# A router's ranking of tokens, cut into four groups instead of three, with four merge steps at each turn

## The chip, the cores and the metric

The kernel runs on one core of one Trainium2 chip. The metric is the device time of one execution in microseconds (us), as the median of several runs. The core has five engines that run side by side, each through its own list of instructions in order: TensorE (PE in the profile), VectorE (DVE), ScalarE (ACT), GpSimd (POOL) and SyncE (SP, which here only issues transfers). Transfers can be issued from SP, ACT and POOL.

## The reference

An encoder of two layers over 1024 tokens of 1024 channels. Each layer mixes tokens, projects the merged result with `w_out`, normalises it, and then lets each of 16 experts take the 128 tokens whose affinity to it is highest:

```python
x = layer_norm(DEEPNORM_ALPHA * x + mix, ln1_g[l], ln1_b[l])      # mix ends with merged @ w_out
...
cap = EC_FACTOR * T // N_EXPERTS                                   # 2 * 1024 // 16 = 128
aff = jax.nn.softmax(jnp.einsum('btd,de->bte', x, w_router).astype(jnp.float32), axis=-1)
gate, idx = lax.top_k(jnp.swapaxes(aff, 1, 2), cap)
xs = jax.vmap(lambda xb, ib: xb[ib])(x, idx)
hid = jax.nn.silu(jnp.einsum('becd,edf->becf', xs, w1)) * jnp.einsum('becd,edf->becf', xs, w3)
ye = jnp.einsum('becf,efd->becd', hid, w2) * gate[..., None].astype(x.dtype)
```

## The kernel before

The program is written out by Python generators, and the order in which they are advanced is the order of the instructions on each engine. `run` advances a main generator; after each of its turns it lets `W.step` load and split a weight piece, and `side_all` advance the work that follows. `side_all` takes one step of each generator in `posts`, and three rounds over the generators in `lows`.

`out_main` is the main generator here. It goes over eight token tiles of 128 tokens; each is projected by 16 turns of three matmuls of 512 columns (the products are split in three for accuracy, lines 325 to 327, output `pz`), and it yields after every second turn. L1269 adds the residual, and L1270 takes statistics. `turned` transposes a half of the tile on TensorE (L1240) and ScalarE copies it (L1242). `post` follows each tile: `ln_mv` finishes the statistics (lines 420 to 422, the last on GpSimd), `logits` (L1287) multiplies by the router's weights, `affinities` (L1294 to L1299) makes the softmax, and `ln_apply` writes the normalised rows, which are then stored twice (L1234, L1235; for the last tile L1234 is issued from ScalarE's queue).

`ln_apply` has a parameter `spread`: that many of the two halves go over ScalarE (L432) and two products on GpSimd (L433, L434); the others take two VectorE instructions (L436, L437).

`topk_stage` ranks. When the tiles of a group are done, two small matmuls put the group's affinities into rows of 64 values (L1343), and ScalarE copies them to a work buffer `tkb` (L1346). Eight rounds of L1354 (the eight largest) and L1357 (take them out) put each row in order. `moved` (L1330) brings rows together through TensorE and PSUM, L1360 or `join` (L1334) fetches them, and `ordered` puts a row in order in seven steps of two instructions (L1321 the larger, L1322 the smaller of each pair). Each `yield` ends a step. `lag` is six empty steps while the tiles still run. `TK` holds the 128 largest of each expert so far. After the last group L1370 takes the threshold, `topk` turns it into places, and the first expert's rows are gathered (L1446), transposed (L1461) and multiplied.

Of the kernel before, what the change touches and what calls it, by code (L numbers as in the profile page):

```python
# [22 lines left out]
NE = 16  # L23
# [60 lines left out]
class Weights:  # L84
    """Streams weight pieces: DMA in, split into two float32r parts."""

# [67 lines left out]
def tile_encoder_trunk(ctx: ExitStack, tc: tile.TileContext, I, out, dbg=None, depth=DEPTH):  # L154
# [23 lines left out]

# [1 line left out]
    cst = cp.tile([128, NCONST], F32, name="cst")  # L180
# [42 lines left out]

# [1 line left out]
    RT = dram([4, 128, RTW], "RT")  # L225
# [11 lines left out]

# [1 line left out]
    names = {}  # L239
# [46 lines left out]

# [1 line left out]
    sides, posts, lows = [], [], []  # L288
# [11 lines left out]
    def side_all():  # L300
        """one step of the first side that is ready, of each tile that follows, and of one of the low ones"""
        for g in list(posts):
            try:
                next(g)
            except StopIteration:
                posts.remove(g)
        for _ in range(3):
            for g in list(lows):
                try:
                    next(g)  # L310
                except StopIteration:
                    lows.remove(g)
        return [side_step(), bool(posts or lows)]
# [14 lines left out]

# [1 line left out]
    def bcast_row(dst, src, off, n, eng=None):  # L330
# [55 lines left out]

# [1 line left out]
    def alloc_xt():  # L388
        """x transposed in two float32r parts: [part][token half][pair of k] -> [128, 2, 512]"""
        return [[[slot([128, 2, 512], F32R, f"x{part}{hf}{i}") for i in range(4)] for hf in range(2)]  # L390
                for part in "hl"]
# [18 lines left out]

# [1 line left out]
    def ln_stats(z, eps):  # L412
# [12 lines left out]
    def ln_apply(zs, mv, g, b, o, spread=1):  # L425
        """halves: one on VectorE, the other shared by ScalarE and GpSimd (spread)"""
        if spread:
            nc.vector.scalar_tensor_tensor(mv[:, 2:3], mv[:, 0:1], -1.0, mv[:, 3:4], op0=OP.mult, op1=OP.mult)  # L428
        for hf in range(2):
            ns = slice(512 * hf, 512 * hf + 512)  # L430
            if spread and hf >= 2 - spread:
                nc.scalar.activation(o[:, ns], zs[hf], AF.Identity, scale=mv[:, 3:4], bias=mv[:, 2:3])  # L432
                nc.gpsimd.tensor_tensor(o[:, ns], o[:, ns], g[:, ns], op=OP.mult)  # L433
                nc.gpsimd.tensor_tensor(o[:, ns], o[:, ns], b[:, ns], op=OP.add)  # L434
            else:
                nc.vector.scalar_tensor_tensor(o[:, ns], zs[hf], mv[:, 0:1], g[:, ns], op0=OP.subtract, op1=OP.mult)  # L436
                nc.vector.scalar_tensor_tensor(o[:, ns], o[:, ns], mv[:, 3:4], b[:, ns], op0=OP.mult, op1=OP.add)  # L437
# [3 lines left out]

    # =====================================================================
    def pair(shape, name, dtype=F32):
        return [slot(shape, dtype, f"{name}{i}") for i in range(2)]

    def transposes_to(yt, src, hf):
        """src [128 t, 4, 256] token-major (half hf of the tokens) -> yt[ct][:, half]"""
        for ct in range(2):
            p = bank("py")
            for k in range(4):  # L450
                nc.tensor.transpose(p[:, 128 * k:128 * k + 128], src[:, k, 128 * ct:128 * ct + 128], ident)
            nc.scalar.copy(yt[ct][:, 512 * hf:512 * hf + 512], p)
        yield
# [77 lines left out]

# [1 line left out]
    def attention(l, L, T):  # L533
# [161 lines left out]

# [1 line left out]
    def mlstm(l, L, T):  # L697
        CV, GB = L["CV"], L["GB"]
        IGF, VV = T.pop("igf"), T.pop("cv")
        pre = [T.pop("cq"), T.pop("ck")]  # L700
        # gate rows [64 (dir, chunk, head), 128]
        nc.vector.tensor_tensor(IGF[:, 1], IGF[:, 1],
# [32 lines left out]
        for j in range(2):  # L735
            nc.tensor.transpose(p[0:1, 64 * j:64 * j + 64], gm[:, j:j + 1], ident[:64, :64])
        # chunk recurrence of the running maximum, rows ordered (dir, head, step)
        cr = sm.tile([1, 5, 64], F32, name="cr", tag="u0", bufs=1)
# [61 lines left out]
        yield  # L800
        # convolution and silu (twice the value), feature-major
        qk = []
# [19 lines left out]
        for hf in range(2):  # L822
# [6 lines left out]
            yield  # L829
        # states at the start of each chunk  # L830
        CS = pair([128, 8, 2, 65], "CS")
# [149 lines left out]

    # =====================================================================
    def mixers_main(l, L, T, XT, rows):
# [144 lines left out]
        del VV, IGF  # L1128
        # gates: tanh(z / 2)
        W.raw_max, W.prep_max = 1, 3  # L1130
# [58 lines left out]
    def out_main(l, L, MG, xsrc, R, nxt):  # L1189
        # the router takes rows before their normalisation: with weights times g, the sum of these, and b's part  # L1190
        CV, gw = L["CV"], L.pop("wr")
# [8 lines left out]
        L.update(gw=gw, gc=gc)  # L1200
        # twice the sum is normalised (MG holds twice the merged branches), with four times the epsilon
        LG = pair([128, D], "lg")
# [9 lines left out]
        def post(t, x, xt, st):  # L1212
            ts = slice(128 * t, 128 * t + 128)
            mv = ln_mv(st, 4.0 * EPS)
            if t == 0:
                p = bank("pl")
                nc.tensor.matmul(p[:, 0:2 * NE], ones, gs.rearrange("p a e -> p (a e)"), start=True, stop=True)
                nc.vector.tensor_copy(gc, p[:, 0:2 * NE].rearrange("p (a e) -> p a e", a=2))
            if t < 7:
                yield  # L1220
            if t == 0:
                turned(x, xt, 0)
                yield
            pl = bank("pl")
            logits(L, xt, pl, 0)
            turned(x, xt, 1)
            if t < 7:
                yield
            logits(L, xt, pl, 1)
            affinities(L, t, pl, mv, R)  # L1230
            for _ in range(6 if t == 7 else 0):
                yield
            ln_apply(halves(x), mv, LG[0], LG[1], x, spread=1 + (t > 5))
            (nc.scalar if t == 7 else nc.gpsimd).dma_start(X1[l][ts, :], x)  # L1234
            nc.gpsimd.dma_start(XA[l][ts, :], x)  # L1235
# [53 lines left out]
    def affinities(L, t, p, mv, R):  # L1289
        """of a token tile, from its rows before normalisation times the router's weights"""  # L1290
        AF_, gc = R[0], L["gc"]
# [7 lines left out]
        nc.vector.tensor_scalar(AF_[:, t, :], AF_[:, t, :], rs[:, 2:3], None, op0=OP.mult)  # L1299
        if t in (3, 5, 7):  # L1300
            lows.append(topk_stage(R, {3: 0, 5: 4, 7: 6}[t], t))

    def topk_stage(R, t0, t):
        """the values of token tiles t0..t: rows of 64 put in order, then rows joined (two rows, one of them
        reversed, fall and rise; the larger of each pair, 128 apart, are the 128 largest of two rows of 128);
        TK holds the 128 largest so far"""
        AF_, TK, stages = R
        nt = t + 1 - t0
        r = NE * nt
# [53 lines left out]
        if t == 7:  # L1363
            while stages[0] != t0:
                yield
            join(3, TK, TB[2], NE)
            q = moved(TB[2][:r], NE, NE)
            yield from ordered(3, NE)
            join(3, TB[4], q, NE)
            nc.vector.tensor_reduce(TK[:, 0:1], TB[3][:NE], axis=AX.X, op=OP.min)  # L1370
            return
# [19 lines left out]
    def topk(l, R):  # L1391
        """1 + place of each token among those its expert takes (0: not taken), ties by the lower index"""
        AF_, mn, _ = R
# [35 lines left out]
    def moe(l, pos, tail):  # L1429
# [67 lines left out]
        def h3_last(e):  # L1497
            """one half of the columns after the other, so that the first is turned behind the second"""
            p3 = [bank("h3"), bank("h3")]
# [108 lines left out]
    def add_first(zs, t):  # L1608
        """a token tile taken to PSUM"""
        p = [bank("pf"), bank("pf")]  # L1610
# [5 lines left out]
    def add_last(tail, t, nf, p, inside):  # L1616
        """what the last expert gives to a token tile, added in PSUM or to the tile"""
        zs, yeh, yel, ohT = tail[:4]
# [7 lines left out]
    def finish(l, tail):  # L1626
        """LN2 of one token tile at a time: statistics run one tile ahead"""
        zs, LG = tail[0], tail[4]
# [41 lines left out]

    # =====================================================================
    for l in range(depth):
# [87 lines left out]
```

The weights of the experts stream through 45 buffers of 512 KB; `W.budget` says how many pieces may be held.

## Time and profile before

| | us |
|---|---|
| median of 3 runs (lowest, highest) | 3269.47 (3265.74, 3276.28) |
| span of the profiled execution | 3270.7 |
| TensorE busy in it | 3073.0 (94%) |
| VectorE busy | 2154.1 (66%) |
| ScalarE busy | 1462.6 (45%) |
| GpSimd busy | 1319.3 (40%) |

The profiled execution is listed by its span alone: 3270.7 us, which lies 1.2 us over the median of the runs and inside their range. Its mean granted TensorE clock is 0.977. The two layers run the same code: the projection of layer 0 ends near 958 us and its first expert product starts at 994 us; in layer 1 the same places are 1612.5 us later. Busy time is a sum over stages with different limits, so what this change does is read from the stretch from 900 to 994 us and its twin.

### The profile page before, as it was taken

The page shows a single profiled execution, that of the slowest core. Times are in us where ns is not written, and L with a number is a line of the kernel's source. Part 1 is how long each engine was busy: PE and PEld are TensorE (multiplying, and loading weights), DVE is VectorE, ACT ScalarE, POOL GpSimd, SP SyncE. Part 2 cuts the span into 40 slices and gives each one's busy share as a digit, 9 for nine tenths or more (in the row PEclk, how much of TensorE's full clock was granted, in tenths as well). Part 3 has the DMA queues.
Part 4 walks back from the last instruction along what each step waited for, and adds up shares of the span by engine and source line. Part 5 has one row for each costly group of instructions (what it writes and reads, how often), then busy time and mean ns, then how long its engine had stood idle before and what let it go on. Part 6 is the DMA issues. An engine that isn't in the chain of part 4 may idle for free. (4 is left out here: it accounts for less than half of the span.)

```text
span 3270.7 us, 45191 instructions
## 1 busy us (share of the span) xinstructions
PE 3073.0 (94%) x15502; PEld 2452.3 (75%) x15502; DVE 2154.1 (66%) x3736; ACT 1462.6 (45%) x2101; POOL 1319.3 (40%) x1244
## 2 busy tenths in 40 slices
PE   8999999999978999999899999999999699999997
PEld 7977787778756777777689787877778477777774
DVE  3435552228679999999962465422385899999898
ACT  3122223332226777777531222233312277777773
POOL 0000011005436777777630000100074377777786
PEclk9999999999988999999999999999999799999998
DMA  4312323238567999999522123331484699999973
GB/s 162 97 33 78 110 90 126 65 105 298 197 238 256 358 356 346 354 360 355 164 94 85 39 84 103 123 100 59 163 297 147 237 338 358 352 351 359 356 286 123
DMA packets 283111, 670.64 MB, mean 205 GB/s; under 512 B 26866, under 2 KB 125258, under 8 KB 282880
## 3 DMA queue, kind: packets, MB, share of 16 engines
q1 hardware_dynamic: 259616, 586.16, 49.4%
q0 software_dynamic: 22976, 80.54, 8.3%
q8 instruction: 122, 2.00, 0.2%
q14 instruction: 109, 0.89, 0.1%
q10 hardware_dynamic: 288, 1.05, 0.1%
HBM read 578.60 MB, written 89.06 MB: 204 GB/s over the span
## 5 line engine op out<-in xcount | busy, mean ns | idle before, releaser
L131 DVE TENSOR_TENSOR wlo<-wraw,whi 128x768 fp32r<-128x768 f32 (+1 forms) x918 | 1161.6, 1296 | 483.9 <-ACT whi L124 456.7
L124 ACT CAST whi<-wraw 128x1024 fp32r<-128x1024 f32 (+1 forms) x922 | 944.2, 1047 | 362.0 <-PE h L326 81.3
L131 POOL TENSOR_TENSOR wlo<-wraw,whi 128x256 fp32r<-128x256 f32 x772 | 857.9, 1183 | 274.5 <-ACT whi L124 231.7
L325 PE MATMUL pb<-xh,whi 128*128 128x512 f32 x1344 | 549.3, 409 | 0.0
L326 PE MATMUL pb<-xl,whi 128*128 128x512 f32 x1344 | 529.5, 394 | 0.0
L327 PE MATMUL pb<-xh,wlo 128*128 128x512 f32 x1344 | 529.3, 394 | 0.0
L326 PE MATMUL h<-wlo,xsT 128*128 128x512 f32 x1024 | 414.6, 405 | 50.7 <-DVE wlo L131 34.2
L325 PE MATMUL h<-whi,xsT 128*128 128x512 f32 x1024 | 416.7, 407 | 0.5 <-ACT xsT L1464 0.5
L327 PE MATMUL h<-whi,xsT 128*128 128x512 f32 x1024 | 406.1, 397 | 5.4 <-DVE xsT L1465 5.4
L325 PEld LDWEIGHTS pb<-xh,whi 128*128 128x128 f32 x1344 | 252.9, 188 | 78.7 <-issue 21.8
L327 PEld LDWEIGHTS pb<-xh,wlo 128*128 128x128 f32 x1344 | 252.7, 188 | 58.7
L326 PEld LDWEIGHTS pb<-xl,whi 128*128 128x128 f32 x1344 | 253.2, 188 | 52.7 <-issue 1.9
L326 PEld LDWEIGHTS h<-wlo,xsT 128*128 128x128 f32 x1024 | 194.6, 190 | 126.1 <-DVE wlo L131 61.3
L1138 ACT ACTIVATE gt<-pb,CVh 128x512 f32<-128x512 f32 x128 | 87.6, 685 | 362.5 <-PE pb L327 341.0
L327 PEld LDWEIGHTS h<-whi,xsT 128*128 128x128 f32 x1024 | 194.2, 190 | 45.0 <-DVE xsT L1465 6.8
L326 PE MATMUL py<-wlo,hT 128*128 128x512 f32 x512 | 208.9, 408 | 19.5 <-POOL wlo L131 15.8
L325 PEld LDWEIGHTS h<-whi,xsT 128*128 128x128 f32 x1024 | 194.3, 190 | 41.3 <-ACT xsT L1464 1.5
L325 PE MATMUL py<-whi,hT 128*128 128x512 f32 x512 | 202.8, 396 | 0.0
L327 PE MATMUL py<-whi,hT 128*128 128x512 f32 x512 | 201.7, 394 | 0.0
L325 PE MATMUL pa<-whi,xh 128*128 128x256 f32 (+1 forms) x640 | 188.7, 295 | 6.7 <-ACT whi L124 5.8
L326 PE MATMUL pa<-wlo,xh 128*128 128x256 f32 (+1 forms) x640 | 186.2, 291 | 2.2 <-DVE wlo L131 2.2
L327 PE MATMUL pa<-whi,xl 128*128 128x256 f32 (+1 forms) x640 | 185.4, 290 | 0.1
(381 smaller groups left out, 4452.1 us busy)
## 6 DMA issues: line engine op xcount, KB each, us to landing
wraw<-in_w_e_dram SPq DMA_DIRECT2D x768, 512.0 KB
wraw<-in_w_in_dram SPq DMA_DIRECT2D x100, 512.0 KB
GD<-gt SPq DMA_DIRECT2D x64, 512.0 KB
gl<-GD SPq DMA_DIRECT2D x64, 512.0 KB
Rb<-RD POOLq DMA_DIRECT2D x32, 256.0 KB, 4.9
wraw<-in_w_branch_dram SPq DMA_DIRECT2D x16, 512.0 KB
wraw<-YT SPq DMA_DIRECT2D x16, 512.0 KB
wraw<-in_w_out_dram SPq DMA_DIRECT2D x16, 512.0 KB
```

The source lines that it names most:

```text
L124: self.nc.scalar.copy(hi, raw)
L131: e.tensor_tensor(lo[c], raw[c], hi[c].bitcast(F32), op=OP.subtract)
L325: nc.tensor.matmul(p, sh, mh, start=first, stop=False)
L326: nc.tensor.matmul(p, sh, ml, start=False, stop=False)
L327: nc.tensor.matmul(p, sl, mh, start=False, stop=last)
L1138: nc.scalar.activation(gt[:, 512 * hf:512 * hf + 512], p, AF.Tanh, scale=0.5, bias=CVh[:, j:j + 1])
```

## The change

`side_all` takes four rounds over `lows` instead of three. The groups of token tiles are 0 to 3, 4 to 5, 6, and 7 instead of 0 to 3, 4 to 5, and 6 to 7; the last group then has 16 rows of 64 for each half instead of 32, so its second joining is gone. The last tile's `ln_apply` stands directly behind its `affinities` (before, six turns later). Tile 6's normalisation goes whole to VectorE (`spread` 0, before 2); tile 7's keeps 2.

```diff
@@ side_all
-        for _ in range(3):
+        for _ in range(4):
             for g in list(lows):
@@ out_main, post
             affinities(L, t, pl, mv, R)
-            for _ in range(6 if t == 7 else 0):
-                yield
-            ln_apply(halves(x), mv, LG[0], LG[1], x, spread=1 + (t > 5))
+            ln_apply(halves(x), mv, LG[0], LG[1], x, spread={6: 0, 7: 2}.get(t, 1))
             (nc.scalar if t == 7 else nc.gpsimd).dma_start(X1[l][ts, :], x)
@@ affinities
-        if t in (3, 5, 7):
-            lows.append(topk_stage(R, {3: 0, 5: 4, 7: 6}[t], t))
+        if t in (3, 5, 6, 7):
+            lows.append(topk_stage(R, {3: 0, 5: 4, 6: 6, 7: 7}[t], t))
@@ topk_stage
             join(3, TK, TB[2], NE)
-            q = moved(TB[2][:r], NE, NE)
-            yield from ordered(3, NE)
-            join(3, TB[4], q, NE)
             nc.vector.tensor_reduce(TK[:, 0:1], TB[3][:NE], axis=AX.X, op=OP.min)
```

The other lines of the diff take out comments. What the generators make of it shows in the instruction lists. Line numbers from 1231 on are smaller by two in the changed kernel (by five from 1370 on).

On VectorE, at token tile 4 of layer 0: the end of the affinities, the normalisation of the half that VectorE takes (`xr`), and what stands behind it. Before:

```order
L1298 RECIPROCAL rs<-rs 128x1
L1299 TENSOR_SCALAR aff<-aff,rs 128x16
L428 SCALAR_TENSOR_TENSOR mv<-mv 128x1
L436 SCALAR_TENSOR_TENSOR xr<-xr,mv,lg_6438 128x512
L437 SCALAR_TENSOR_TENSOR xr<-xr,mv,lg_6439 128x512
L1269 SCALAR_TENSOR_TENSOR xr<-xr,pz 128x512
L1270 BN_STATS st<-xr 128x6
L1360 COPY tkb<-pl 64x64
L1321 TENSOR_TENSOR tkb<-tkb 64x64
```

The same place in the changed kernel:

```order
L1297 TENSOR_SCALAR aff<-aff,rs 128x16
L428 SCALAR_TENSOR_TENSOR mv<-mv 128x1
L436 SCALAR_TENSOR_TENSOR xr<-xr,mv,lg_6438 128x512
L437 SCALAR_TENSOR_TENSOR xr<-xr,mv,lg_6439 128x512
L1319 TENSOR_TENSOR tkb<-tkb 64x8x8
L1320 TENSOR_TENSOR tkb<-tkb 64x8x8
L1319 TENSOR_TENSOR tkb<-tkb 64x16x4
L1320 TENSOR_TENSOR tkb<-tkb 64x16x4
L1319 TENSOR_TENSOR tkb<-tkb 64x32x2
L1320 TENSOR_TENSOR tkb<-tkb 64x32x2
L1319 TENSOR_TENSOR tkb<-tkb 64x64
L1320 TENSOR_TENSOR tkb<-tkb 64x64
```

The first group's copy and first three steps have moved ahead of tile 4's affinities, and its last four steps now stand right behind the normalisation.

On TensorE, at token tile 6 of layer 0, behind the tile's logits (L1287 before, L1285 in the changed kernel): the projection of tile 7 (`pz`) and the small matmuls of the ranking. Before:

```order
L1287 MATMUL pl<-wr,xt 128x16 x4
L325 MATMUL pz<-whi,mh 128x512
L326 MATMUL pz<-wlo,mh 128x512
L327 MATMUL pz<-whi,ml 128x512
L325 MATMUL pz<-whi,mh 128x512
L326 MATMUL pz<-wlo,mh 128x512
L327 MATMUL pz<-whi,ml 128x512
L1330 MATMUL pl<-tkb,cst 32x64
L325 MATMUL pz<-whi,mh 128x512
```

In the changed kernel, from the end of the six products behind the same logits on:

```order
L1341 MATMUL pl<-cst,aff 16x64 x2
L325 MATMUL pz<-whi,mh 128x512
L326 MATMUL pz<-wlo,mh 128x512
L327 MATMUL pz<-whi,ml 128x512
L325 MATMUL pz<-whi,mh 128x512
L326 MATMUL pz<-wlo,mh 128x512
L327 MATMUL pz<-whi,ml 128x512
L1328 MATMUL pl<-tkb,cst 16x128
L325 MATMUL pz<-whi,mh 128x512
```

Tile 6's own affinities are now turned into rows here (L1341), and six products later stands the second joining of tiles 4 and 5 (L1328, 16x128), which before stood behind the whole projection. In the same way the first group's joining to 32 rows (32x128) now stands twelve products behind tile 4's logits; before it stood behind tile 5's transposes. Its row of 16x128 has moved up from behind tile 5's affinities to the stretch behind tile 5's first transposes. The rows of tiles 0 to 3 and of tiles 4 and 5 (L1343) are made six products behind their tile's logits, before twelve.

On ScalarE, at the end of the ranking of layer 0: the last tile's affinities, its normalisation, its store and the copy of the last group's rows. Before:

```order
L1297 ACTIVATE aff,rs<-rs 128x16
L1346 COPY tkb<-pl 64x64
L432 ACTIVATE xr<-xr,mv 128x512 x2
L1234 DMA X_115<-xr 128x1024
L124 CAST whi<-wraw 128x1024 x3
```

In the changed kernel:

```order
L1295 ACTIVATE aff,rs<-rs 128x16
L432 ACTIVATE xr<-xr,mv 128x512 x2
L1232 DMA X_115<-xr 128x1024
L1348 COPY tkb<-pl 16x64 x2
L124 CAST whi<-wraw 128x1024 x3
```

The copies from which the last group is put in order now stand behind the store of the normalised rows.

## Rows read from the trace of the kernel before

**Rows 1.** Windows: busy us of PE, PEld, DVE, ACT, POOL; clock, DMA share

```profile
899.80:961.50 61.70, 57.39 (x289) 45.63 (x289) 43.26 (x159) 13.13 (x31) 26.28 (x30) 0.94 0.57 212
935.40:941.10 5.70, 5.70 (x14) 4.46 (x14) 3.77 (x26) 0.00 (x0) 0.60 (x2) 0.50 0.47 184
2549.40:2552.30 2.90, 2.90 (x8) 2.27 (x7) 2.90 (x24) 0.00 (x0) 0.05 (x1) 0.50 0.91 362
981.50:994.10 12.60, 5.09 (x42) 4.17 (x42) 10.15 (x30) 1.63 (x2) 3.13 (x4) 0.50 0.15 43
1040.00:1560.00 520.00, 491.92 (x2267) 380.87 (x2265) 479.95 (x574) 391.46 (x433) 398.37 (x353) 1.00 0.98 355
```

**Rows 2.** TensorE's waits from 895 to 995 us: total us, times, longest

```profile
PE pl L1330 <- DVE tkb L1322: 10.1, 2, 7.1
...
PE pq L1240 <- DVE xr L1269: 0.7, 1, 0.7
```

**Rows 3.** Timeline of VectorE, tiles 4 and 5: start us, us, then the instruction

```profile
914.15 0.23 DVE L1294 SCALAR_TENSOR_TENSOR rs<-gc,mv,pl 128x16 f32<-128x16 f32 x1 [2.76 <-PE pl L1287]
...
917.27 0.68 DVE L1269 SCALAR_TENSOR_TENSOR xr<-xr,pz 128x512 f32<-128x512 f32 x1
...
932.02 1.28 DVE L1321 TENSOR_TENSOR tkb<-tkb 32x64 f32<-32x64 f32 x1
...
934.57 0.21 DVE L1322 TENSOR_TENSOR tkb<-tkb 32x64 f32<-32x64 f32 x1
```

**Rows 4.** Timeline of TensorE, tiles 4 and 5

```profile
913.97 0.48 PE L325 MATMUL pz<-whi,mh 128*128 128x512 f32 x1
...
915.21 0.39 PE L327 MATMUL pz<-whi,ml 128*128 128x512 f32 x1
...
934.92 0.58 PE L1330 MATMUL pl<-tkb,cst 32*16 32x128 f32 x2 [2.95 <-DVE tkb L1322]
```

**Rows 5.** Timeline of VectorE, tiles 5, 6 and 7

```profile
930.57 0.75 DVE L436 SCALAR_TENSOR_TENSOR xr<-xr,mv,lg 128x512 f32<-128x512 f32 x1
...
949.30 0.23 DVE L1294 SCALAR_TENSOR_TENSOR rs<-gc,mv,pl 128x16 f32<-128x16 f32 x1 [2.56 <-PE pl L1287]
...
950.75 0.23 DVE L1299 TENSOR_SCALAR aff<-aff,rs 128x16 f32<-128x16 f32 x1
...
957.69 0.21 DVE L1321 TENSOR_TENSOR tkb<-tkb 32x64 f32<-32x64 f32 x1
...
958.07 0.21 DVE L1321 TENSOR_TENSOR tkb<-tkb 32x64 f32<-32x64 f32 x1
```

**Rows 6.** Timeline of VectorE behind the last affinities

```profile
963.02 0.23 DVE L1299 TENSOR_SCALAR aff<-aff,rs 128x16 f32<-128x16 f32 x1
...
964.02 0.22 DVE L1354 MAX8 tkb<-tkb 64x8 f32<-64x64 f32 x1 [0.21 <-ACT tkb L1346]
...
969.99 0.21 DVE L1354 MAX8 tkb<-tkb 64x8 f32<-64x64 f32 x1
...
970.77 0.21 DVE L1360 COPY tkb<-pl 32x64 f32<-32x64 f32 x1 [0.45 <-PE pl L1330]
...
977.83 0.28 DVE L1334 TENSOR_TENSOR tkb<-TK,tkb 16x128 f32<-16x128 f32 x1
...
981.20 0.27 DVE L1370 TENSOR_REDUCE TK<-tkb 16x1 f32<-16x128 f32 x1
```

**Rows 7.** Timeline of ScalarE, tiles 6 and 7

```profile
951.14 1.52 ACT L432 ACTIVATE xr<-xr,mv 128x512 f32<-128x512 f32 x2 [0.61 <-issue]
...
971.52 1.52 ACT L432 ACTIVATE xr<-xr,mv 128x512 f32<-128x512 f32 x2 [7.53 <-DVE mv L428]
977.61 0.35 ACTq L1234 DMA_DIRECT2D X<-xr  x1
978.00 1.99 ACT L124 CAST whi<-wraw 128x1024 fp32r<-128x1024 f32 x2 [4.96 <-POOL xr L434]
```

**Rows 8.** Waits of SyncE's queue from 960 to 1040 us: total us, times, longest

```profile
SPq L103 <- DVE wlo L131: 37.4, 9, 28.1
```

## Prediction

> **What bounds the stretch now.** I first cut the execution into windows [rows 1]. While the last projection runs (899.8 to 961.5 us) TensorE is busy for 57.39 of 61.7 us: its queue sets the pace, and whatever makes it wait is lost. In the ranking behind it nearly nothing runs on TensorE, and the reader sees one chain instead: VectorE's merges up to the threshold, the places, the gather, and the first expert product at 994 us. The experts follow at 491.92 busy of 520 us. Next I read who makes TensorE wait near the ranking [rows 2]: its joinings (L1330) wait for the merges twice, 7.1 us at the end, where nothing else could run, and 2.95 us in the middle of the projection (the 10.1 less the 7.1), where products stand behind. The timelines [rows 3 to 7] say what each of these waits is made of. Layer 1 repeats layer 0, so every term counts twice.
>
> **The projection.** The lists show that the ranking's small matmuls now come earlier in TensorE's queue, so the question for each is whether VectorE has its rows ready. TensorE takes its matmuls in order: in the 2.95 us wait no product was run [rows 4].
>
> *The joining to 32 rows* now stands twelve products behind tile 4's logits. Tile 4's affinities begin on VectorE at 914.15, and the next row behind the normalisation starts at 917.27 [rows 3]. There the changed list has the last four merge steps. Two of them fall beside GpSimd's two products of that tile: the same situation at tile 5 took from 932.02 to 934.78, so 2.76 us for two pairs [rows 3], where a pair alone takes 0.38 (957.69 to 958.07) [rows 5]. VectorE is done at 917.27 + 2.76 + 0.76 = 920.79, and TensorE starts 0.14 later, as at 934.92 behind 934.78 [rows 3, 4]. Its own twelve products start at 913.97, at 0.25 a step (six of them up to 915.21) [rows 4], so that the twelfth ends near 917.1. New wait: 3.8 us. What goes is the 2.95 us of the joining to 16 rows: it now stands 24 products (6.0 us at 0.25) behind the one to 32, while VectorE needs seven pairs at 0.38 and tile 5's residual row (2.7 and some 1.4) for it.
>
> *The second joining of tiles 4 and 5*, before the first thing behind the projection, now stands twelve products behind tile 6's logits, and tile 6's normalisation is whole on VectorE in front of the merges it needs. Affinities at 949.30, their last row at 950.75; two such rows of 512 take 1.45 (930.57 to 932.02), four 2.9; then four pairs, no GpSimd product beside them, 1.5 [rows 3, 5]. With 0.15 for the end of the affinities VectorE is done at 955.3, and TensorE starts at 955.5. By tile 4's spacing its first six products are through at 950.8; it waits 0.3 for tile 6's affinities, takes 0.35 for L1343, and is through with the next six at 953.0. New waits: 0.3 + 2.5 = 2.8 us. What is late next is tile 7's projection.
>
> *Smaller terms.* Tiles 3 and 5 have their L1343 six products earlier too, at 0.35 of wait each: 0.7. Two more small groups lie inside the projection; taken at 0.35 each (bounds nothing, and the 0.58 that one takes [rows 4]): 0.7. The 0.7 us that tile 7's transposes waited for L1269 [rows 2] go, since VectorE is now ahead there. Ten merge rows now stand between the last statistics and their sum, 1.4 us at 0.14 each (42 rows from the first to the eighth maximum, 5.97 us [rows 6]); most hides behind the logits: 0.5.
>
> *The clock.* After its 2.95 us wait TensorE was granted 0.50, the lower level of 1.2 GHz, in layer 0 for 14 products in 5.70 us, in layer 1 for 8 in 2.90 [rows 1]. At 0.25 a product these lost 2.2 and 0.9 us. Now two waits of that kind stand in a layer instead of one. I add one such fall at 2.2, the larger, since the first wait is longer than the old one; bounds nothing and 3.5 (two of 2.2 less the old 0.9).
>
> Sum of the projection: 3.8 - 2.95 + 2.8 + 0.7 + 0.7 - 0.7 + 0.5 + 2.2 = 7.05 us later per layer.
>
> **Behind the last affinities.** Call the start of their last row X, before 963.02; the threshold was at 981.20, 18.2 later [rows 6]. Removed are the last joining, its seven steps and its maximum, 977.83 to 981.20 less one joining of 0.3: 3.1 us. Also, the seven pairs from 970.77 on ran beside GpSimd's products of tile 7 and took 6.8 us instead of 2.7, so 4.1 more [rows 6].
>
> Yet the copy from which the last group is sorted now stands behind the store of tile 7's rows in ScalarE's queue, and that store waits for the products. Before, ScalarE's half of the normalisation began at 971.52, the store was issued at 977.61, and its next instruction ran at 978.00, after 4.96 us of idling: 6.48 in all [rows 7]. The half began 0.39 behind the affinities at tile 6 (950.75, 951.14) [rows 5, 7]. So the copies run at X + 6.9, and the first maximum at X + 7.3, where before it was X + 1.0. From it the list has 37 rows to the eighth at 0.142: X + 12.6; 0.78 to the copy behind the joining (969.99 to 970.77); then fourteen rows at 0.14, four pairs alone at 0.38, one joining 0.3: threshold at X + 17.2. So 1.0 us earlier. The products' price is gone only because VectorE now waits while they run. Bounds: had all of the removed 3.1 and 4.1 come back without the later start, 7.2 earlier; with ScalarE's copies and the mixed rows a tenth slower, nothing.
>
> Here a page weighs otherwise. The row has ScalarE idle for 4.96 us behind a store [rows 7]. The Trainium skill, "DMA: Bandwidth & Descriptors", section "Issuing engines are not separate DMA queues", says that issuing from several engines only saves a sequencer the time of issuing, small beside the transfer. Read so, the place of a store in a queue would cost its 0.35 us alone; by the row it costs the whole wait in front of it, and the sum by the page's reading is the second rival's below. This trace speaks against reading it so.
>
> **Sum.** 7.05 - 1.0 = 6.05 us per layer, 12.1 in all. Against the profiled span of 3270.7: 3282.8. The median of the runs is 1.2 lower, so the forecast is **3281.6 us**, 0.37% slower. The places, the gather and the experts follow unchanged.
>
> **Rivals.**
> - *The experts take it up* (3269.5, no change). They move 355 GB/s at a DMA share of 0.98 while TensorE has 28 us idle [rows 1]; were the weight stream the pace, a later start would cost nothing. Against it: the buffers are full by then. SyncE's queue waits up to 28.1 us for a split piece [rows 8], and the DMA share is 0.15 in the last 12.6 us before the experts [rows 1], so the stream starts again only with them. It decides if weights still flow in that window. Chance 0.09.
> - *ScalarE isn't held by the store* (3278.4, within the bound below). The copies come at X + 1.9 and the first maximum 5.0 earlier, but some 4.2 us of GpSimd's products then lie beside the merges; before, about 5.0 of them cost 4.1 [rows 6, 7], so 3.4 come back. 1.6 better per layer. It decides if the copies start before GpSimd's last product ends. Chance 0.07.
> - *TensorE finds its rows ready* (not slower). If VectorE ended the four steps of tile 4 before 917.1 and those of tile 6 before 953.0, the 3.8, the 2.5 and their clock go, and so do the old 2.95 and its mean 1.5 of clock: 7.05 - 3.8 - 2.5 - 2.2 - 1.5 = -2.95, with the tail -3.95 per layer, 3261.6. For it: before, the joining to 32 rows met no wait. Against it: VectorE would have to be 3.7 us faster over 6.6. Chance 0.10.
> - *Worse* (3285 to 3292). The clock at its bound, 1.3 more per layer, and the tail at nothing, 1.0 more: 3286, and above if the lower clock lasts over both waits. Chance 0.13.
>
> **How the numbers follow.** A run of this kernel tells about 0.3%, 9.8 us, from no change. The forecast has 0.61, its own range is 3276 to 3288, and about four fifths of it lies over 3279.3. Slower: 0.49 + 0.13 = 0.62. The rest of the forecast (0.12), the first two rivals and 0.06 of the third: 0.34 within. Faster by more, if the third comes with some of the 7.2 us of the tail's bound: 0.04. The range of 3272 to 3289 leaves out the first rival, the third and the top of the worse case, about 0.2.
>
> **What would show it.** Right: waits of L1328 (32x128) near 3.8 us at tile 5 and (16x128) near 2.5 us at tile 7, none of the old one; a clock of 0.50 behind both; ScalarE idle near 5 us at its store and then two copies, with the first maximum over 6 us behind the last affinities; no merge row of 1.2 us near the end. Wrong: the first expert product less than 2 us later behind the projection's start than before, or a maximum that starts before GpSimd's products end. What would most easily break the sum is the clock, whose falls in the two layers differ by half already.

## The result and the profile after

The changed kernel takes 3288.64 us (median of 4 runs, 3285.20 to 3291.49) against 3268.38 of the kernel before: ratio 1.0057, 95% interval 1.0042 to 1.0071. It is slower, and by more than the forecast of 3281.6. The profiled execution has a span of 3283.4 us (12.7 more than before) and a time of 3285.2.

The windows answer to [rows 1]; the first is the projection, then the first products behind the two new waits in layer 0 and in layer 1, and the experts.

```profile
897.80:964.55 66.75, 57.19 (x294) 44.84 (x293) 51.24 (x212) 11.77 (x31) 20.64 (x26) 0.97 0.60 224
920.40:922.60 2.20, 2.20 (x6) 1.80 (x6) 2.04 (x9) 0.00 (x0) 0.00 (x0) 0.50 0.94 378
954.70:957.30 2.60, 2.60 (x12) 2.17 (x12) 2.32 (x12) 0.15 (x1) 0.00 (x0) 1.00 0.98 336
2539.40:2544.30 4.90, 4.90 (x12) 3.80 (x12) 3.34 (x17) 0.00 (x0) 0.00 (x0) 0.50 0.54 209
2574.80:2578.50 3.70, 3.70 (x10) 2.94 (x10) 2.39 (x12) 0.16 (x1) 0.00 (x0) 0.54 1.00 355
...
1043.00:1563.00 520.00, 491.47 (x2267) 381.52 (x2266) 478.12 (x574) 391.88 (x434) 400.63 (x353) 1.00 0.97 355
```

TensorE does the same work in the projection (57.19 us busy, before 57.39) in a stretch that is 5 us longer. The experts are as before, so nothing is taken up there. Who made TensorE wait, from 893 to 998 us (total, times, longest), answers to [rows 2]:

```profile
PE ptx L1456 <- DMA xs<-X,idx: 6.0, 1, 6.0
...
PE pl L1328 <- DVE tkb L1320: 3.9, 1, 3.9
PE pl L1341 <- DVE mv L428: 2.8, 3, 2.1
PE pl L1328 <- DVE tkb L1346: 2.5, 1, 2.5
...
PE pq L1238 <- DVE xr L1267: 1.2, 1, 1.2
```

The wait of 2.95 us is gone, and two stand in its place. Their making, in the timeline of VectorE at tile 4 (the third row ends its last merge pair before the joining) and at tile 6, then of TensorE at both places; they answer to [rows 3, 4]. For the second wait the profile names L1346, a row of 0.11 us that clears the next group's buffer directly behind that pair.

```profile
916.26 1.28 DVE L1319 TENSOR_TENSOR tkb<-tkb 64x64 f32<-64x64 f32 x1
...
917.71 1.17 DVE L1319 TENSOR_TENSOR tkb<-tkb 64x64 f32<-64x64 f32 x1
...
919.58 0.21 DVE L1320 TENSOR_TENSOR tkb<-tkb 64x64 f32<-64x64 f32 x1
...
954.04 0.21 DVE L1320 TENSOR_TENSOR tkb<-tkb 32x64 f32<-32x64 f32 x1
```

```profile
919.85 0.63 PE L1328 MATMUL pl<-tkb,cst 64*32 64x128 f32 x2 [3.87 <-DVE tkb L1320]
...
954.39 0.37 PE L1328 MATMUL pl<-tkb,cst 32*16 32x128 f32 x2 [2.52 <-DVE tkb L1346]
```

The last row of the waits, 1.2 us at the transposes of tile 7 (L1238), looks like the 0.7 us of [rows 2], but it stands at another place. Before, the transposes of the first half waited, 0.68 us up to 956.74. In the changed kernel those start at once (first row, cut after three of the four), and the ones of the second half wait:

```profile
958.26 0.49 PE L1238 MATMUL pq<-cst,xr 128*128 128x128 f32 x3
...
961.81 0.66 PE L1238 MATMUL pq<-cst,xr 128*128 128x128 f32 x4 [1.22 <-DVE xr L1267]
```

Behind the last affinities the timeline of ScalarE, then of VectorE (they answer to [rows 6, 7]):

```profile
966.45 1.52 ACT L432 ACTIVATE xr<-xr,mv 128x512 f32<-128x512 f32 x2 [0.61 <-issue]
972.54 0.34 ACTq L1232 DMA_DIRECT2D X<-xr  x1
972.98 0.41 ACT L1348 COPY tkb<-pl 16x64 f32<-16x64 f32 x2 [5.01 <-POOL xr L434]
```

```profile
966.07 0.23 DVE L1297 TENSOR_SCALAR aff<-aff,rs 128x16 f32<-128x16 f32 x1
...
973.43 0.22 DVE L1352 MAX8 tkb<-tkb 48x8 f32<-48x64 f32 x1 [6.42 <-ACT tkb L1348]
...
978.97 0.21 DVE L1352 MAX8 tkb<-tkb 48x8 f32<-48x64 f32 x1
...
983.47 0.27 DVE L1365 TENSOR_REDUCE TK<-tkb 16x1 f32<-16x128 f32 x1
```

ScalarE stands still for 5.01 us in front of its two copies, the first maximum comes 7.36 us behind X (the start of the last affinities' last row), the threshold 17.40 behind it, where it was 18.18 [rows 6].

What the prediction took as unchanged has changed too: the gather. In the timeline of before, the row that makes its indices and the gather on GpSimd, then the same rows of after with VectorE's split (L131) that follows, and the first transposes of the gathered rows:

```profile
987.45 0.16 DVE L1444 SCALAR_TENSOR_TENSOR idx<-ax 128x1 int32<-128x1 f32 x1
...
987.91 1.05 POOL L1446 DMA_INDIRECT xs<-X,idx  x1 [9.42 <-DVE ax L1449]
```

```profile
989.72 0.16 DVE L1439 SCALAR_TENSOR_TENSOR idx<-ax 128x1 int32<-128x1 f32 x1
...
990.26 4.82 DVE L131 TENSOR_TENSOR wlo<-wraw,whi 128x768 fp32r<-128x768 f32 x3
990.73 1.41 POOL L1441 DMA_INDIRECT xs<-X,idx  x1 [17.32 <-DVE ax L1445]
...
995.49 1.97 PE L1456 MATMUL ptx<-cst,xs 128*128 128x128 f32 x8 [6.00 <-DMA xs<-X,idx]
```

The gather starts 1.01 us behind its indices (before 0.46) and takes 1.41 us (1.05). From the threshold to the first transposes it is 12.02 us in both layers, where it was 11.11 and 11.37.

So that all kernels can be set beside each other, I cut each profiled execution at the same rows: **A** from the last affinity row of tile 3 to that of tile 7 (before 61.53 us in layer 0, 60.58 in layer 1; given below as the difference to that), **B** from there (X) to the threshold, **C** from the threshold to the first transposes. Each pair is layer 0 / layer 1. A holds the clock, which differs between executions: in the profile of before, 13 products at the lower clock stand behind its wait in layer 0 and 7 in layer 1 (a product of 512 columns counts from 0.60 us on). The ratio is that of the runs' times to those of before, measured beside them.

| kernel | A, us more than before | B, us | C, us | ratio (95%) |
|---|---|---|---|---|
| before | 0 / 0 | 18.18 / 18.18 | 11.11 / 11.37 | 1 |
| changed | +5.03 / +8.13 | 17.40 / 17.37 | 12.02 / 12.02 | 1.0057 (1.0042 to 1.0071) |
| three_rounds | +0.63 / +2.50 | 21.01 / 21.00 | 12.15 / 12.07 | 1.0038 (1.0024 to 1.0052) |
| before_four_rounds | +3.58 / +5.14 | 16.20 / 16.20 | 11.42 / 11.06 | 1.0022 (1.0013 to 1.0032) |
| before_four_groups | +0.98 / +2.81 | 19.34 / 19.33 | 12.27 / 12.23 | 1.0026 (1.0014 to 1.0037) |
| before_norms | -1.94 / +0.26 | 20.14 / 20.12 | 11.34 / 11.21 | 1.0013 (1.0003 to 1.0022) |
| store_gpsimd | +7.11 / +8.07 | 14.93 / 14.93 | 12.30 / 11.98 | 1.0047 (1.0034 to 1.0061) |
| later_joinings | +0.23 / +1.69 | 19.32 / 19.28 | 12.20 / 12.02 | 1.0033 (1.0021 to 1.0046) |
| before_later_joining | -5.72 / -4.77 | 18.18 / 18.18 | 11.60 / 11.25 | 0.9968 (0.9956 to 0.9980) |
| filled_waits | +4.70 / +5.14 | 17.39 / 17.38 | 12.03 / 12.19 | 1.0056 (1.0043 to 1.0070) |
| filled_again | +4.19 / +5.17 | 17.41 / 17.37 | 12.08 / 12.09 | one time, 3288.99 us |
| spare_buffer | +6.64 / +8.03 | 17.39 / 17.37 | 11.44 / 11.10 | one time, 3289.49 us |

### The profile page after: what moved, and what is told of

Same layout as the page of the kernel before. It is cut to its first block, busy times and chain, and to the rows that moved or that the text cites. A ratio compares the mean times of both kernels' runs of the same rounds, so it can differ in the third digit from the quotient of the medians.

```text
span 3283.4 us, 45295 instructions
## 1 busy us (share of the span) xinstructions
PE 3074.0 (94%) x15510; PEld 2451.8 (75%) x15510; DVE 2156.6 (66%) x3822; ACT 1460.2 (44%) x2103; POOL 1315.0 (40%) x1236
## 3 DMA queue, kind: packets, MB, share of 16 engines
q10 hardware_dynamic: 288, 1.05, 0.1%
## 5 line engine op out<-in xcount | busy, mean ns | idle before, releaser
L131 DVE TENSOR_TENSOR wlo<-wraw,whi 128x768 fp32r<-128x768 f32 (+1 forms) x918 | 1162.1, 1296 | 487.9 <-ACT whi L124 458.5
L131 POOL TENSOR_TENSOR wlo<-wraw,whi 128x256 fp32r<-128x256 f32 x772 | 864.2, 1190 | 272.3 <-ACT whi L124 233.0
```

The source lines that it names most:

```text
L131: e.tensor_tensor(lo[c], raw[c], hi[c].bitcast(F32), op=OP.subtract)
```

## The experiments

My theory was that of the prediction: the joinings stand too early in TensorE's queue, and the tail's gain is eaten by the copies behind ScalarE's store. The first rival: the loss comes from the norms and the store, not from TensorE's queue. A second: VectorE's work is the bound, and TensorE's queue only shows where it is waited for.

**One part at a time.** Four kernels have one part of the change undone or done alone.

*three_rounds*, from the changed kernel:

```diff
-        for _ in range(4):
+        for _ in range(3):
             for g in list(lows):
```

> The changed kernel with three rounds over the side work instead of four; the groups and the norms stay as changed. Theory (TensorE waits at the joinings that four rounds moved forward): the joining to 32 rows goes back to its old place, 21 + 9 products behind tile 4's logits, so the waits of 3.87 us and 2.52 us and the slow products behind them are gone and the old wait of 2.95 us is back; the projection ends within 0.7 us of where it ended before. The tail has 97 VectorE rows from the last affinities to the threshold instead of 70, and it still starts behind ScalarE's store: 27 more rows at 0.14 us, 3.8 us, of which some lie in the 5 us in which VectorE waited; threshold near X + 20. Some 2.5 us later than before per layer, ratio 1.0016 (3273 us), clearly under the 1.0057 of the changed kernel. Rival (the place of the norm and its store is the cost, not the waits of TensorE): the tail is no better than in the changed kernel and the ratio stays at 1.005 or above.

Its waits of TensorE, of 888 to 990 us, and its threshold (X is at 956.15):

```profile
PE ptx L1456 <- DMA xs<-X,idx: 6.1, 1, 6.1
...
PE pl L1328 <- DVE tkb L1320: 3.0, 1, 3.0
```

```profile
977.16 0.28 DVE L1365 TENSOR_REDUCE TK<-tkb 16x1 f32<-16x128 f32 x1
```

The two new waits are gone, the old one is back, and A is 4.4 and 5.6 us shorter than in the changed kernel: that part of the theory holds. (That A is 2.50 us longer than before in layer 1, where 0.7 was expected, goes with 12 products at the lower clock instead of 7 and 0.6 us more of waits at the transposes.) B is 1 us longer than I had expected, X + 21.0: the merges that three rounds leave undone lie behind the last affinities. The whole fell between theory and rival, 1.0038.

*before_four_rounds*, the same line of the kernel before turned from 3 to 4:

> The kernel before with four rounds over the side work instead of three, nothing else. Theory: this alone brings the wait of 3.8 us at the joining to 32 rows and takes the old 2.95 us one away; tile 6's norm goes over ScalarE and GpSimd here, so VectorE has the rows of the second joining near 953 us and TensorE waits for them 0 to 1.3 us instead of 2.5; threshold still near X + 18. 1.5 to 4 us later per layer, ratio 1.001 to 1.0025 (3272 to 3277 us). Rival (the second wait and the norms carry the whole loss): ratio within 0.0005 of 1.

A is 3.6 and 5.1 us longer (waits of 3.9 and 1.4 us at L1330, the second just over the 0 to 1.3 expected), B 2.0 shorter, more than expected: the fourth round also gets merges done before the last affinities. 1.0022 lies in the expected range.

*before_four_groups*, from the kernel before:

```diff
-        if t in (3, 5, 7):
-            lows.append(topk_stage(R, {3: 0, 5: 4, 7: 6}[t], t))
+        if t in (3, 5, 6, 7):
+            lows.append(topk_stage(R, {3: 0, 5: 4, 6: 6, 7: 7}[t], t))
...
-            q = moved(TB[2][:r], NE, NE)
-            yield from ordered(3, NE)
-            join(3, TB[4], q, NE)
```

> The kernel before with the groups 0-3, 4-5, 6 and 7 instead of 0-3, 4-5 and 6-7, nothing else: three rounds, norms as before. Theory: TensorE's queue in the projection is as before but for one more small group, 0.35 us; behind the last affinities stand 97 VectorE rows instead of 79, since tile 6's merge into the best 128 is not done while the projection runs, but one trip through TensorE fewer: threshold at X + 19 to X + 20.5 instead of X + 18.2. 1 to 2.7 us later per layer, ratio 1.0006 to 1.0016. Rival (the joining that goes is a gain of 3.1 us per layer whatever the rounds): ratio 0.998.

B is in the expected range (X + 19.3) and not better, so the joining that goes is no gain at three rounds. C is 1.2 and 0.9 longer: the gather's price comes with the four groups. That, and A, put the ratio above the range, at 1.0026.

*before_norms*, from the kernel before:

```diff
-            for _ in range(6 if t == 7 else 0):
-                yield
-            ln_apply(halves(x), mv, LG[0], LG[1], x, spread=1 + (t > 5))
+            ln_apply(halves(x), mv, LG[0], LG[1], x, spread={6: 0, 7: 2}.get(t, 1))
```

> The kernel before with the changed norms alone: the last tile's norm directly behind its affinities, tile 6's norm whole on VectorE; three groups and three rounds. Theory: the copies of the last group stand behind ScalarE's store, so the first maximum starts at X + 7.3 instead of X + 1.0; the seven pairs that lay beside GpSimd's products give 4.1 us back; threshold at X + 20.2 instead of X + 18.2, the projection within 0.5 us of before, no new wait of the gather. 1.5 to 2.5 us later per layer, ratio 1.0009 to 1.0015. Rival (the norms are the larger part of the change's loss): ratio 1.003 or above.

First maximum at X + 7.1, threshold at X + 20.1, ratio 1.0013: as expected, and the first rival falls, as the norms and the store are the smallest part. A is 1.94 us shorter in layer 0, where it was to stay within 0.5: 7 products are at the lower clock instead of 13, and the 0.7 us wait at the transposes is gone. The three parts alone (norms, four rounds, four groups) give 0.13, 0.22 and 0.26%, 0.61 together, against 0.57 for the change: no part gains by itself, and together they don't either. The largest of them is the four groups, which my theory had not named: A, B and C are all longer with them.

**The store.** *store_gpsimd*, from the changed kernel:

```diff
-            (nc.scalar if t == 7 else nc.gpsimd).dma_start(X1[l][ts, :], x)
+            nc.gpsimd.dma_start(X1[l][ts, :], x)
```

> The changed kernel with the last tile's store (L1232) issued from GpSimd's queue, as for the other tiles, instead of ScalarE's. Theory (the copies of the last group stand behind a store that waits for GpSimd's products): ScalarE's idle 5 us before the copies are gone, the copies run near X + 1.9 and the first maximum near X + 2.3 instead of X + 7.3; some merge pairs of tile 6 then lie beside the products (1.2 us rows come back), and the threshold comes 1.6 to 3 us earlier per layer: 3.2 to 6 us less than the changed kernel, ratio near 1.0043. TensorE's waits of 3.87 and 2.52 us stay. Rival (ScalarE is held by something else): first maximum and ratio unchanged.

Timeline of ScalarE and VectorE; X is at 968.17:

```profile
969.98 0.40 ACT L1348 COPY tkb<-pl 16x64 f32<-16x64 f32 x2
970.41 0.22 DVE L1352 MAX8 tkb<-tkb 48x8 f32<-48x64 f32 x1 [1.30 <-ACT tkb L1348]
...
972.05 1.29 DVE L1320 TENSOR_TENSOR tkb<-tkb 16x64 f32<-16x64 f32 x1
```

The 5 us of idling are gone, the first maximum is at X + 2.24, merge rows of 1.29 us come back beside GpSimd's products, and the threshold is 2.47 us earlier than in the changed kernel (14.93 against 17.40). The theory's numbers hold. The time alone would not show it, as 1.0047 and the changed kernel's 1.0057 lie in each other's intervals. In layer 0 the clock took the gain back: 21 products at the lower clock instead of 5 go with an A that is 2.1 us longer.

**The place of the joinings.** *later_joinings*, from the changed kernel (`lag` gets a length):

```diff
-        def lag():
-            for _ in range(6 if len(stages) == 1 else 0):
+        def lag(m=6):
+            for _ in range(m if len(stages) == 1 else 0):
...
             n //= 2
-            yield from lag()
+            yield from lag({(0, 32): 17, (4, 16): 14}.get((t0, n), 6))
```

> The changed kernel with more empty steps ahead of two joinings: 17 instead of 6 ahead of the first group's joining to 32 rows, 14 instead of 6 ahead of the second joining of tiles 4 and 5. Theory (these two joinings make TensorE wait because they stand too early in its queue): the waits of 3.87 and 2.52 us and the slow products behind them, 6.4 us and some 2 us of clock per layer, are gone; VectorE has no less to do, so one or two waits of 1 to 1.5 us for the residual row show at the transposes instead. 4 to 7 us earlier per layer than the changed kernel: 3274 to 3280 us, ratio to the kernel before 1.001 to 1.003. Rival (VectorE's work is the bound, TensorE's order only shows where it is waited for): the same time is lost at other places, ratio 1.005 or above.

Waits of TensorE from 893 to 995 us, and VectorE behind the last affinities (961.12):

```profile
PE pq L1238 <- DVE xr L1267: 3.3, 3, 1.3
PE pl L1341 <- DVE mv L428: 2.2, 2, 1.8
```

```profile
968.49 0.22 DVE L1352 MAX8 tkb<-tkb 48x8 f32<-48x64 f32 x1 [6.43 <-ACT tkb L1348]
...
980.44 0.28 DVE L1365 TENSOR_REDUCE TK<-tkb 16x1 f32<-16x128 f32 x1
```

Both joinings now find their rows, and A is 4.8 and 6.4 us shorter. But 3.3 us of waits for the residual row (L1267) stand where the changed kernel had 1.2, VectorE's own work, and the merges that were put off come back in B, 1.9 us longer. The second rival is right about that half. A, B and C together are 2.7 and 4.5 us better per layer than in the changed kernel, less than the 4 to 7 expected in layer 0, and 1.0033 lies just over the expected range and under the rival's 1.005.

*before_later_joining*, the kernel before with `lag` given a length in the same way and this call:

```diff
             n //= 2
-            yield from lag()
+            yield from lag(14 if (t0, n) == (0, 16) else 6)
```

> The kernel before with 14 empty steps instead of 6 ahead of the first group's joining to 16 rows, so that it stands 18 products and four transposes later in TensorE's queue, 4.9 us at their spacing, more than the 2.95 us that it waits now. Theory: the 2.95 us wait and the slow products behind it (2.2 us lost in layer 0, 0.9 in layer 1) are gone and nothing takes their place, since the later merges have until the next group: 3.9 to 5.2 us earlier per layer, 3260 to 3263 us, ratio 0.9972. Rival: the steps that come later hold the next rows up and the wait comes back at the transposes or behind the last affinities, ratio above 0.999.

The timeline of TensorE at the joining, and the window of its projection (columns as in [rows 1]):

```profile
933.95 0.39 PE L1330 MATMUL pl<-tkb,cst 32*16 32x128 f32 x2
934.26 0.50 PE L325 MATMUL pz<-whi,mh 128*128 128x512 f32 x1
934.60 0.40 PE L326 MATMUL pz<-wlo,mh 128*128 128x512 f32 x1
```

```profile
897.00:953.00 56.00, 54.72 (x289) 43.38 (x289) 43.44 (x160) 13.13 (x31) 26.33 (x30) 1.00 0.61 220
```

No wait at the joining, the full clock through the whole projection, A 5.7 and 4.8 us shorter, B the same 18.18: here VectorE had the time, and the joining only stood too early. At 3259.5 us, 0.9968, this one number beats both kernels.

**The clock.** *filled_waits* and *filled_again* are one program, from the changed kernel:

```diff
-        def moved(src, lo, n):
+        def moved(src, lo, n, fill=0):
             p = bank("pl")
+            for _ in range(fill):
+                nc.tensor.transpose(p[:, 0:128], ident, ident)
...
-            join(i + 1, TB[i], moved(TB[i][:2 * n], n, n), n)
+            join(i + 1, TB[i], moved(TB[i][:2 * n], n, n, {(0, 32): 40, (4, 16): 25}.get((t0, n), 0)), n)
```

> The changed kernel with 40 transposes of a constant put on TensorE ahead of the first group's joining to 32 rows and 25 ahead of the second joining of tiles 4 and 5; their results are overwritten and nobody reads them. At 0.09 us each they take 3.6 and 2.25 us of the waits of 3.87 and 2.52 us. Theory (the lower clock behind a wait comes from TensorE having nothing to run): the joinings run at the same moments, no product behind them is slow, and 1 to 3.7 us of clock per layer come back: 2 to 7 us less than the changed kernel, ratio 1.0035 to 1.005. Rival (the clock falls whatever TensorE does there): the slow products stay, ratio 1.0055 or above.

> The kernel with the filled waits a second time, for its profile: the first profile showed no slow product in the two projections and the shortest of five times, 3278.0 us, while the others went up to 3289.4. Theory (the lower clock comes from waiting, and falls elsewhere differ from one execution to the next): again no slow product between the projection's start and its end in either layer; a longer time shows slow products or waits elsewhere. Rival (the first profile was an exception): slow products stand behind the filled waits again.

In layer 0 of the first, VectorE's last row before the joining, and TensorE's timeline (cut at 912.80, so that only part of the 40 shows):

```profile
916.17 0.21 DVE L1320 TENSOR_TENSOR tkb<-tkb 64x64 f32<-64x64 f32 x1
```

```profile
912.80 4.09 PE L1328 MATMUL pl<-cst 128*128 128x128 f32 x36
916.82 0.40 PE L1330 MATMUL pl<-tkb,cst 64*32 64x128 f32 x2
917.16 0.50 PE L325 MATMUL pz<-whi,mh 128*128 128x512 f32 x1
917.50 0.39 PE L326 MATMUL pz<-wlo,mh 128*128 128x512 f32 x1
```

The fill took more than forecast: 36 transposes in 4.09 us are 0.11 us each, not 0.09, so the 40 outlast the wait, and the joining starts 0.44 us behind VectorE's last row, where in the changed kernel it is 0.06 (919.85 behind 919.79). With TensorE kept running, no product of either projection is at the lower clock, in either execution; behind the waits of the changed kernel there were 5 and 0 in layer 0, 11 and 8 in layer 1. A is 0.3 to 0.8 us shorter in layer 0 and 3.0 in layer 1, with the late joining paid out of it. That shows the cause of the lower clock at these places. The times don't show it: they go from 3278.0 to 3289.4 us with the median at 1.0056. The two profiles tell why they can't: A, B and C are the same within 0.5 us, while the spans are 3276.2 and 3287.2. The 11 us lie outside the ranking: tile 3's last affinity row comes 5.4 us later in layer 0 and 11.4 in layer 1, at a mean granted clock of 0.977 instead of 0.979.

**The gather.** *spare_buffer*, from the changed kernel, ahead of the last group's work buffer:

```diff
+        if t == 7:
+            spare = slot([128, 8, 128], F32, "tkb")
+            nc.vector.memset(spare[:, 0, 0:1], 0.0)
+            del spare
         tb = slot([128, 8, 128], F32, "tkb")
```

> The changed kernel with one more buffer taken and given back at the start of the last group (one column of it is set to zero), which turns the buffers by one place; the gathered rows then lie in another buffer, and in the gather's list of waits TensorE's no longer stands behind VectorE's. Theory (the added wait of the gather costs): the gather starts near 0.46 us behind the row that makes its indices and takes 1.05 us, as in the kernel before, instead of 1.0 and 1.41, and the first transposes of an expert start 11.1 to 11.4 us behind the threshold instead of 12.0. Rival (the longer idling of GpSimd, or the state of the transfers): 12.0 us stay.

The first gather in the instruction lists of before, of the changed kernel, and of this one:

```
196 L1446 DMA xs<-X_115,idx 128x1024 [waits DMASW5_49,DMASW4_49,DMASW7_49,DMASW2_49,DMAHW6_49,DMASW1_49,DVE_49]
192 L1441 DMA xs<-X_115,idx 128x1024 [waits DMASW4_49,DMASW7_49,DMASW1_49,DMAHW3_49,DVE_49,PE_49]
192 L1445 DMA xs<-X_115,idx 128x1024 [waits DMASW7_49,DMASW4_49,DMAHW3_49,DMASW1_49,DVE_49]
```

```profile
991.89 0.16 DVE L1443 SCALAR_TENSOR_TENSOR idx<-ax 128x1 int32<-128x1 f32 x1
992.34 1.05 POOL L1445 DMA_INDIRECT xs<-X,idx  x1 [16.77 <-DVE ax L1448]
```

0.45 us and 1.05 us are back, and C is 11.44 and 11.10. GpSimd idled 16.77 us before it, so the idling is not the cause. All twelve profiles fall in two kinds, the same in both layers: in five kernels (before, before_four_rounds, before_norms, before_later_joining and this one) the gather starts some 0.45 us behind its indices and takes 1.05; in the other seven, all with four groups, it starts 0.96 to 1.01 us behind and takes 1.40 to 1.46. What turned the gather is the buffer that its rows go to, with the wait on TensorE that comes with it; the extra wait and the buffer were not tried apart.

## Why the prediction was right, and where not

**The joinings: right.** 3.8 us forecast at the one to 32 rows, 3.87 and 3.86 measured in the two layers; 0.3 + 2.5 at tile 6, 0.29 + 2.52 measured; the old wait gone; two merge rows beside GpSimd's products at 1.28 and 1.17 us, as at tile 5 in [rows 3]. later_joinings and three_rounds show that their place in the queue makes them.

**The 0.7 us of tile 7's transposes: failed.** VectorE was ahead at the first half, as forecast, and that wait went. But at the second half a wait came that the sum puts at nothing: 1.22 us in layer 0 and 0.71 in layer 1. There VectorE was not ahead: the maxima and merges of tile 6 fill it up to the residual row. The term is +0.5 and 0.0 us instead of -0.7.

**The clock: mis-sized.** I added one fall of 2.2 us per layer. By the rows above, 12 products take 4.90 us at a granted clock of 0.50 and 2.60 at 1.00, so a product at the lower clock loses 0.2 us (the prediction's 0.25 a product at the full clock was too long). At that price layer 0 has 5 instead of 13, 1.6 us less, and layer 1 has 19 instead of 7, 2.4 more: 0.4 on the mean. The 2.52 us wait made the clock fall in layer 1 but not in layer 0. On the mean this term was 1.8 us too dear and the one before it 1.0 too cheap, and that the projection's sum stands all the same (7.05 forecast, 5.03 and 8.13 measured, 6.6 on the mean) is luck.

**The tail: right.** First maximum at X + 7.36 (7.3 forecast), threshold at X + 17.40 (17.2), a gain of 0.8 us instead of 1.0. store_gpsimd shows that the store holds the copies. The Trainium skill, "DMA: Bandwidth & Descriptors", section "Issuing engines are not separate DMA queues", says that issuing from several engines at once only saves a sequencer the time of issuing. The reading of it that the prediction weighed, that a store's queue costs nothing else, is contradicted at this place: the queue of one store is worth 2.47 and 2.44 us of the threshold in the two layers.

**"The places, the gather and the experts follow unchanged": failed at the gather,** 0.91 and 0.65 us later; the experts are unchanged.

**The sum: near, and partly by luck.** For both layers, the projection was forecast at 14.1 us and measured 13.2, the tail at -2.0 and measured -1.6, the gather at nothing and measured 1.6: 12.1 forecast, 13.1 measured, and the two spans differ by 12.7. What the clock was too dear (3.6) is what the transposes and the gather were too cheap (2.0 and 1.6).

**The step from the span to the median: failed.** I took the median 1.2 us below the span of 3270.7. A run's time lies 1.8 us over its span (3285.2 to 3283.4 in the changed kernel), so the profiled execution of before took some 3272.5 us, 4 over the median. By the sum of 12.1 us an execution like it would take 3284.6; the profiled one of the changed kernel took 3285.2, but it is the quickest of its four, 3.4 us under their median. So 7 of the 20 us between the medians are not in the two profiles at all, and no term of the prediction stands for them. filled_again shows that executions of one program differ by 11 us outside the ranking; whether the change makes the longer ones more frequent stays open.

**The rivals.** The experts took up nothing. ScalarE was held by the store. TensorE didn't find its rows ready. The time lies in the range of the "worse" case, but not by its mechanism: the clock was below its term and the tail gained.

## What to carry to other kernels

A small matmul that waits for another engine holds all work behind it, so its place in TensorE's queue is chosen by when its rows are ready: moving one joining 18 products back gave 0.32% here, while starting the side work sooner lost time. A step that is put off comes back later, so the gain is counted behind the last stage as well. And a copy that others wait for doesn't belong behind a store that waits.

## What the runs showed that I had not expected

A wait of 2.5 us was followed by the lower clock in five of six places (two layers of the changed kernel, store_gpsimd and spare_buffer), with 7 to 13 products at 0.63 us; in the sixth, layer 0 of the changed kernel, the next twelve products keep 1.00. Of the other waits at joinings in the projections of the twelve profiles, all 16 of 2.9 to 3.9 us were followed by it, with 5 to 13 products, and the two of 1.4 us in before_four_rounds were not.

A copy with one input is held by GpSimd's products too. On VectorE in the changed kernel, beside the products of tile 5:

```profile
936.41 1.31 DVE L1378 COPY TK<-tkb 16x128 f32<-16x128 f32 x1
```

In layer 1 it takes 1.31 us again; other copies of this shape, with no such product beside them, take 0.20 us (L1383). The Trainium skill, "SBUF — State Buffer", section "Who interferes with whom", lists copies among the operations that can take the port pair that VectorE and GpSimd share; this row agrees. The slower gather also runs beside VectorE: the split starts 0.47 us ahead of it (990.26 and 990.73), where in the kernels with the quick gather it starts 0.08 us behind. That the split is what slows it is not shown, since no run here took the split away.

One buffer more in the rotation was worth 0.6 to 0.9 us per layer: the wait list of an instruction far from the edit had changed.
